# Hybrid decoder step: five early block results held in DRAM, sums of x built sooner, sixteen two-block groups where there were fifteen

## The chip, the cores and the metric

One core of a Trainium2 chip runs one launch of the kernel. The metric is device time in microseconds (us), the median of the runs; less is better. The engines are called as in the profile: PE does matmuls, DVE, ACT and POOL do elementwise work, SP issues most DMAs. Each engine takes its own instructions strictly in the order written in the program.

## The reference, cut to what matters

A prompt of 16 meta tokens and 512 new tokens and a group of 8 single-token samples pass through one layer with shared weights: 536 token columns, 2048 features.

```python
xn = rmsnorm(x, norm_gain)
h = jnp.einsum('btd,de->bte', xn, w_in)
q, k, v, z_a, u, z_s, g_a, g_s = jnp.split(h, IN_SPLITS, axis=-1)
# q, k, v -> sliding-window attention with sinks -> o_attn;  u -> S5 state space scan, gelu, GLU -> y_ssm
br_a = (o_attn * jax.nn.silu(z_a)) @ w_attn_out
br_s = (y_ssm * jax.nn.silu(z_s)) @ w_ssm_out
return x + (jax.nn.sigmoid(g_a) * br_a + jax.nn.sigmoid(g_s) * br_s) @ w_out
```

All is float32. The change touches how the 48 blocks of 128 features of g_s (numbers 0 to 15), z_s (16 to 23), z_a (24 to 31) and g_a (32 to 47) are computed, and in which order.

## The kernel before, in words

**Split matmuls.** Each float32 operand is split in a high and a low part (`whi`, `wlo`, `xh`, `xl`), and a product is three matmuls: high by high, high by low, low by high. A weight *unit* is 1024 input features by 128 output features, 512 KB: SP loads `raw`, ACT casts `whi`, DVE subtracts `wlo`. The token columns come as two halves of 260 (268 with the meta columns), so each matmul streams 260 columns.

**Plain blocks and groups.** A plain block (`xblock`, `mm`) is two units: 2 units, 8 slices, 3 products, 2 halves, 96 matmuls of 260 columns. A group (`Quads`, `quad`) computes two blocks by a Strassen-like scheme: 7 products of 8 slices by 3, 168 matmuls of 260 columns, where two plain blocks take 192. It needs sums of the weights (made on DVE, line 1073) and sums of the halves of x (`tau`, made by `taus`: x is loaded again as `xg`, scaled on ACT, added up in `T` on DVE, then cast on ACT and subtracted on DVE, eight times).

**Stages.** (1) While x and the first weights arrive, PE computes the first three blocks together (line 1255); ACT squares x for the norm. (2) A chain of small steps makes the row scale `R`: PE sums the squares (`wg<-ones,acc`), DVE takes an inverse square root (lines 559 to 564), writes five small diagonal matrices `dg`, PE spreads each with a matmul against ones, DVE copies `R`. Meanwhile PE goes on with two more blocks. The results of these five early blocks stay in SBUF (`keep`, the tiles `xr` of the pool `xld`) until `R` is there; then `evac` multiplies them by `R`, applies the gate function (for 16 to 31: a tanh on ACT and one more DVE step) and writes them to `gD` in DRAM. (3) Four plain blocks (`NA`). `taus` runs beside them. (4) Fifteen groups (`NQ`). (5) `ORDER1`: one plain block, then eight blocks of u and twelve of q, k and v in turn, with the state space scan beside them on DVE, ACT and PE. (6) Seven plain blocks, then a last one that is written out apart, with attention beside them; (7) the GLU, the two branch products, the output product in eight groups.

**What sets the order.** `XORDER` says which block is computed when. Side work is a set of generators (`bg.add`), of which a few steps are written after every few matmuls. A scheduler then fixes the order on each engine at build time; `high_priority` pulls steps forward. The tiles `z` and `t` of the pool `ev` are rings of two buffers each: a third `z` waits until the DMA that reads the first has ended. The weights run through rings of three `raw`, three `whi` and three `wlo`.

Of the kernel before, what the change touches and what calls it, by code (L numbers as in the profile page):

```python
# [8 lines left out]
F32 = mybir.dt.float32  # L9
# [544 lines left out]
def rsqrt_dve(nc, pool, out, v_, shape, tag, end="t", iters=3):  # L554

    v = nc.vector
    t = pool.tile(shape, F32, name=tag + end)
    oi, vi = out.bitcast(I32), v_.bitcast(I32)
    v.tensor_scalar(out=oi, in0=vi, scalar1=1, scalar2=None, op0=ALU.arith_shift_right)
    v.tensor_scalar(out=oi, in0=oi, scalar1=-1.0, scalar2=1597463007.0, op0=ALU.mult, op1=ALU.add)  # L560
    for _ in range(iters):
        v.tensor_tensor(out=t, in0=v_, in1=out, op=ALU.mult)
        v.scalar_tensor_tensor(out=t, in0=t, scalar=-0.5, in1=out, op0=ALU.mult, op1=ALU.mult)  # L563
        v.scalar_tensor_tensor(out=out, in0=t, scalar=1.5, in1=out, op0=ALU.add, op1=ALU.mult)
# [111 lines left out]
class Attn:  # L676
# [228 lines left out]
    def sample(self, oD):  # L905
# [14 lines left out]
        for e in range(2):  # L920
# [168 lines left out]
def trunk(tc, A, O):  # L1089
# [89 lines left out]
    def mm_x(w0, **kw):  # L1179
        return mm(2, lambda k, c: xk(xh, k, c, w0), lambda k, c: xk(xl, k, c, w0), w0, **kw)  # L1180
# [26 lines left out]
        nc.sync.dma_start(out=gD[i], in_=flat(z))  # L1207


    with tc.tile_pool(name="xld", bufs=2, side="right") as xld:  # L1210
        ones = xld.tile([P, P], F32, name="ones", bufs=1)
        v.memset(ones, 1.0)

        wt = aux.tile([P, 512], F32, name="tr")
        for _ in range(NWARM):
            nc.tensor.matmul(wt[:, 0:P], lhsT=ones, rhs=ones, start=True, stop=True)
        acc = xld.tile([P, 2, CH], F32, name="acc", bufs=1)
        def square(kt):
            sq = acc if kt == 0 else xld.tile([P, 2, CH], F32, name="xsq")
            nc.scalar.activation(out=sq, in_=xrs[kt], func=AF.Square)  # L1220
            if kt:
                v.tensor_tensor(out=acc, in0=acc, in1=sq, op=ALU.add)

        def keep(i, ps):

            t = xld.tile([P, 2, CH], F32, name="xr", bufs=NXR)
            with tc.high_priority(offset=HIGH):
                nc.scalar.copy(out=t[:, :, 0:260], in_=ps)
            early.append((i, t[:, :, 0:260]))

        xrs, early = [], []
        NB0 = 3
        ps3 = [aux.tile([P, 2, 512], F32, name="aux")] + [mmp.tile([P, 2, 512], F32, name="mm") for _ in range(2)]
        gain = cst.tile([P, 16], F32, name="gain")
        pieces = {0: 1, 1: 1, 2: 2, 4: 4, 8: 4, 12: 4}
        for kt in range(16):
            xr = xld.tile([P, 2, CH], F32, name="xr", bufs=NXR)
            xrs.append(xr)
            nc.sync.dma_start(out=xr, in_=A["x"][:, kt])
            if kt == 0:  # L1240
                nc.sync.dma_start(out=gain, in_=A["gain"])
            if kt % 8 == 0:
                first = ws.made
                w3 = [ws.tiles(first + j) if kt == 0 else ws.tiles(first + j, xld) for j in range(NB0)]
                ws.made = ws.i = first + NB0
            kp = xkeep(kt, xr, None)
            next(kp)
            for j in range(NB0):
                if kt in pieces:
                    ws.piece(first + j, w3[j], slice(kt % 8, kt % 8 + pieces[kt]))  # L1250
            next(kp)
            for (_, wh, wl), ps in zip(w3, ps3):
                for (wt, xo, f, l) in ((wh, xh, kt == 0, False), (wh, xl, False, False), (wl, xh, False, kt == 15)):
                    for c in range(2):
                        nc.tensor.matmul(ps[:, c, 0:260], lhsT=wt[:, kt % 8], rhs=xk(xo, kt, c, 8), start=f, stop=l)  # L1255
# [4 lines left out]
        early.sort(key=lambda e: e[0])  # L1260
        square(14)
        square(15)
        idn = const("idn")

        af = acc.rearrange("p c w -> p (c w)")
        rp = [aux.tile([P, 512], F32, name=n) for n in ("tr", "wg")]
        toks = [(i, 128 * i, min(128, 2 * CH - 128 * i)) for i in range(5)]
        var = xld.tile([P, 5], F32, name="var", bufs=1)
        rt = xld.tile([P, 5], F32, name="rt", bufs=1)
        v.memset(var, 1.0)  # L1270
        for i, t0, n in toks:
            nc.tensor.matmul(rp[1][0:n, 32 + i:33 + i], lhsT=af[:, t0:t0 + n], rhs=ones[:, 0:1], start=True, stop=True)
        for sl, n in ((slice(0, 4), P), (slice(4, 5), 24)):
            v.tensor_scalar(out=var[0:n, sl], in0=rp[1][0:n, 32 + sl.start:32 + sl.stop], scalar1=1.0 / 2048, scalar2=1e-6,
                            op0=ALU.mult, op1=ALU.add)
        rsqrt_dve(nc, xld, rt, var, [P, 5], "rx")
        Rf = R_.rearrange("p c w -> p (c w)")
        for i, t0, n in toks:
            dg = xld.tile([P, P], F32, name="dg")
            v.tensor_scalar(out=dg[0:n, 0:n], in0=idn[0:n, 0:n], scalar1=rt[0:n, i:i + 1], scalar2=None, op0=ALU.mult)  # L1280
            nc.tensor.matmul(rp[i // 4][:, t0 % 512:t0 % 512 + n], lhsT=ones[0:n], rhs=dg[0:n, 0:n], start=True, stop=True)
        v.tensor_copy(out=Rf[:, 0:512], in_=rp[0])
        v.tensor_copy(out=Rf[:, 512:536], in_=rp[1][:, 0:24])
        for i in range(NB0, NB0 + 2):
            keep(i, mm_x(8))
        for i, t in early:
            evac(XORDER[i], t)
        nx = NB0 + 2
    C = {"idn": idn}
    e32, dsk, bglu, smc = const("e32"), const("dsk"), const("bglu"), const("smc")  # L1290

# [142 lines left out]
        step()  # L1434


    tauc = tc.tile_pool(name="tau", bufs=1, side="right")
    tau = tauc.__enter__()
    tbc = tc.tile_pool(name="tb", bufs=1, side="right")
    tb = tbc.__enter__()  # L1440
    tt = [tau.tile([P, 2, 4, 260], F32R, name=f"tau{p}") for p in range(8)]

    def taus():
        xgs = []

        def load(p):
            if p < 8:
                xgs.append(tb.tile([P, 2, 2, CH], F32, name="xg", bufs=4))
                with tc.issue_after(bg.last):
                    nc.sync.dma_start(out=xgs[p], in_=A["x"][:, 2 * p:2 * p + 2])  # L1450

        for p in range(3):
            load(p)
        yield 0.0
        for p in range(8):
            load(p + 3)
            xg = xgs[p]
            for k in range(2):
                nc.scalar.activation(out=xg[:, k], in_=xg[:, k], func=AF.Copy, scale=gain[:, 2 * p + k:2 * p + k + 1])
            T = tb.tile([P, 4, 260], F32, name="T", bufs=2)  # L1460
            b = xg.rearrange("p k c w -> p (k c) w")[:, :, 8:CH]
            v.tensor_tensor(out=T[:, 0:3:2], in0=b[:, 0:4:3], in1=bc(b[:, 1], 1, 2), op=ALU.subtract)
            v.scalar_tensor_tensor(out=T[:, 1], in0=T[:, 0], scalar=-1.0, in1=b[:, 3], op0=ALU.mult, op1=ALU.subtract)
            v.tensor_tensor(out=T[:, 3], in0=T[:, 1], in1=b[:, 2], op=ALU.add)
            nc.scalar.copy(out=tt[p][:, 0], in_=T)
            yield 1.6
            v.tensor_tensor(out=tt[p][:, 1], in0=T, in1=tt[p][:, 0].bitcast(F32), op=ALU.subtract)
            yield 1.2
    bg.add(taus())
    qs = Quads(tc, nc, A["w"], ws.i + 2 * NA, NQ, wp, 3, 2)  # L1470
    ws.limit = qs.first
    for i in range(NA):
# [357 lines left out]
def _layout(i):  # L1830
# [28 lines left out]
    n0 = 5 + NA  # L1859
# [90 lines left out]
```

## Time and profile before

| what | before |
|---|---|
| median of 3 runs | 1264.08 us (1263.49 to 1266.17) |
| span of the profiled execution | 1262.3 us |
| PE busy | 1250.9 us, 99% |
| DVE busy | 980.6 us, 78% |
| ACT busy | 628.7 us, 50% |
| HBM traffic over the span | 173 GB/s |

For the profiled execution the page gives the span, first to last instruction; a run's time holds in addition what lies around the span. Matmuls are pipelined: the duration of one (283 ns in mean in the groups) is its way through the array, and the next starts long before it ends. What a matmul costs is the distance from start to start, which a row of the chain of waits gives as its length over its count.

### The profile page before, as it was taken

The page shows a single profiled execution, that of the slowest core. Times are in us where ns is not written, and L with a number is a line of the kernel's source. Part 1 is how long each engine was busy: PE and PEld are TensorE (multiplying, and loading weights), DVE is VectorE, ACT ScalarE, POOL GpSimd, SP SyncE. Part 2 cuts the span into 40 slices and gives each one's busy share as a digit, 9 for nine tenths or more (in the row PEclk, how much of TensorE's full clock was granted, in tenths as well). Part 3 has the DMA queues.
Part 4 walks back from the last instruction along what each step waited for, and adds up shares of the span by engine and source line. Part 5 has one row for each costly group of instructions (what it writes and reads, how often), then busy time and mean ns, then how long its engine had stood idle before and what let it go on. Part 6 is the DMA issues. An engine that isn't in the chain of part 4 may idle for free.

```text
span 1262.3 us, 26537 instructions
## 1 busy us (share of the span) xinstructions
PE 1250.9 (99%) x10357; PEld 1227.7 (97%) x10357; DVE 980.6 (78%) x1554; ACT 628.7 (50%) x1344; POOL 266.1 (21%) x437
## 2 busy tenths in 40 slices
PE   9999999999999999999999999999999999999998
PEld 9999999999999999999999999999999999999998
DVE  8687878887778668888897377899887577887875
ACT  8554445444545586556432235567555333344342
POOL 0003999940000033122220123211011000000000
PEclk9999999999999999999999989999999999999999
DMA  8544343443434656555554775777666756555441
GB/s 294 199 160 153 134 143 110 143 150 134 151 126 146 214 172 182 159 165 167 156 159 121 246 211 182 224 240 225 189 214 203 258 174 189 165 192 163 145 139 51
DMA packets 108001, 219.22 MB, mean 174 GB/s; under 512 B 21932, under 2 KB 47492, under 8 KB 107844
## 3 DMA queue, kind: packets, MB, share of 16 engines
q1 hardware_dynamic: 99172, 198.53, 48.5%
q0 software_dynamic: 8704, 19.00, 5.6%
q8 instruction: 81, 1.33, 0.4%
q14 instruction: 44, 0.36, 0.1%
HBM read 181.57 MB, written 36.82 MB: 173 GB/s over the span
## 4 chain that ended last, share of the span: by engine, by line
PE 92%; DVE 3%; DMA 2%; ACT 1%; SPq 1%; issue 0%; DVEq 0%; ACTq 0%
PE mm L1168 45%; PE pr L1382 35%; PE wg L854 2%; PE mm L1255 2%; PE aux L1382 1%; PE aux L1168 1%; PE aux L1255 1%; DVE wlo L1009 1%; PE aux L806 1%; PE aux L805 1%; ACT ct L346 1%; PE tr L526 1%; PE tr L836 1%; PE wg L526 1%; DMA Y<-yD 0%
## 5 line engine op out<-in xcount | busy, mean ns | idle before, releaser
L1075 DVE TENSOR_TENSOR wlo<-raw,whi 128x1024 fp32r<-128x1024 f32 x161 | 198.5, 1253 | 69.6 <-ACT whi L1074 69.0
L1074 ACT CAST whi<-raw 128x1024 fp32r<-128x1024 f32 x161 | 166.4, 1049 | 167.2 <-DVE raw L1073 80.0
L1168 PE MATMUL mm<-xh,whi 128*128 128x260 f32 (+1 forms) x792 | 185.8, 288 | 3.1 <-DVE t L563 2.9
L1008 ACT CAST whi<-raw 128x1024 fp32r<-128x1024 f32 (+3 forms) x128 | 122.3, 965 | 132.3 <-PE mm L1168 85.6
L1168 PE MATMUL mm<-xh,wlo 128*128 128x260 f32 (+1 forms) x792 | 184.4, 287 | 0.0
L1168 PE MATMUL mm<-xl,whi 128*128 128x260 f32 (+1 forms) x792 | 184.1, 286 | 0.0
L1009 DVE TENSOR_TENSOR wlo<-raw,whi 128x1024 fp32r<-128x1024 f32 (+3 forms) x128 | 142.2, 1119 | 46.5 <-ACT whi L1008 45.7
L1382 PE MATMUL pr<-tau,whi 128*128 128x260 f32 x928 | 168.6, 283 | 0.0
L1382 PE MATMUL pr<-cb,whi 128*128 128x260 f32 x848 | 153.0, 283 | 0.0
L1382 PEld LDWEIGHTS pr<-tau,whi 128*128 128x128 f32 x928 | 143.0, 188 | 0.0
L1168 PEld LDWEIGHTS mm<-xh,whi 128*128 128x128 f32 x792 | 132.5, 189 | 5.8 <-ACT KH L747 3.1
L1168 PEld LDWEIGHTS mm<-xl,whi 128*128 128x128 f32 x792 | 133.1, 190 | 0.4 <-issue 0.4
L1168 PEld LDWEIGHTS mm<-xh,wlo 128*128 128x128 f32 x792 | 132.2, 189 | 0.4 <-issue 0.4
L1382 PEld LDWEIGHTS pr<-cb,whi 128*128 128x128 f32 x848 | 130.8, 188 | 0.2 <-ACT z L1416 0.2
L1382 PE MATMUL pr<-tau,wlo 128*128 128x260 f32 x464 | 130.8, 282 | 0.0
L1382 PE MATMUL pr<-cb,wlo 128*128 128x260 f32 x424 | 119.1, 283 | 0.2 <-DVE wlo L1075 0.2
L1073 DVE TENSOR_TENSOR raw<-raw 128x1024 f32<-128x1024 f32 x91 | 113.9, 1252 | 1.6
L1168 PE MATMUL mm<-Y,whi 128*128 128x260 f32 x576 | 105.1, 287 | 0.0
L1382 PE MATMUL pr<-xl,whi 128*128 128x260 f32 x352 | 98.9, 283 | 0.0
L1382 PE MATMUL pr<-xh,wlo 128*128 128x260 f32 x352 | 98.8, 283 | 0.0
L1382 PE MATMUL pr<-xh,whi 128*128 128x260 f32 x352 | 97.1, 283 | 0.0
L1382 PEld LDWEIGHTS pr<-tau,wlo 128*128 128x128 f32 x464 | 87.2, 188 | 0.0
(421 smaller groups left out, 2974.9 us busy)
## 6 DMA issues: line engine op xcount, KB each, us to landing
raw<-in_w SPq DMA_DIRECT2D x202, 512.0 KB, 4.3
gD<-z SPq DMA_DIRECT2D x34, 260.0 KB, 4.3
t<-gD SPq DMA_DIRECT2D x32, 260.0 KB, 3.1
cache<-in_vc POOLq DMA_DIRECT2D x16, 286.0 KB, 3.5
cache<-in_kc POOLq DMA_DIRECT2D x15, 288.0 KB, 4.0
xr<-in_x SPq DMA_DIRECT2D x16, 268.0 KB, 6.5
xg<-in_x SPq DMA_DIRECT2D x8, 536.0 KB, 4.7
sbw<-rawD SPq DMA_DIRECT2D x16, 260.0 KB, 5.1
```

What stands on the lines that cost most here:

```text
L346: nc.scalar.activation(out=dst, in_=src, func=AF.Copy, scale=x)
L526: nc.tensor.matmul(o[n], lhsT=D["CL"][:, 2 * e + n, i, 1:5], rhs=H[:, 2 * e + n, i, 0:140], start=False, stop=(i == 1))
L805: nc.tensor.matmul(ps[:, e, 0:272], lhsT=q, rhs=KH[:, k0:k0 + 272], start=True, stop=False)
L854: nc.tensor.matmul(pv[64 * e:64 * e + 64, 0:256], lhsT=V, rhs=pr[:, e::2], start=(i == 0), stop=(i == len(parts) - 1))
L1008: nc.scalar.copy(out=hi, in_=raw)
L1009: self.dve = nc.vector.tensor_tensor(out=lo, in0=raw, in1=hi.bitcast(F32), op=ALU.subtract).ins
L1073: nc.vector.tensor_tensor(out=o, in0=o, in1=i, op=ALU.add)
L1074: nc.scalar.copy(out=hi, in_=t)
L1075: nc.vector.tensor_tensor(out=lo, in0=t, in1=hi.bitcast(F32), op=ALU.subtract)
L1168: m = nc.tensor.matmul(ps[:, c, 0:W], lhsT=wt[:, k], rhs=xo(kt, c), start=f, stop=l)
L1255: nc.tensor.matmul(ps[:, c, 0:260], lhsT=wt[:, kt % 8], rhs=xk(xo, kt, c, 8), start=f, stop=l)
L1382: m = nc.tensor.matmul(bank, lhsT=wt[:, p], rhs=x(p, e), start=first and f and p == 0, stop=l and p == 7, skip_group_check=not first and l ...
```

## The change

Three things are changed together.

1. **The five early results go to DRAM.** `keep` copies a result into a `z` or `t` tile of `ev` and writes it to a new DRAM tensor `eD`. They are read back, scaled and gated in stage 5, one before each of the second to the sixth item of `ORDER1`.
2. **`taus` comes sooner.** Its pools open after the first three blocks, so it is written beside the two blocks of stage 2. The pool `xld` closes there; the small tiles of the norm are now in a pool `xsm` with one buffer each, also `dg`, which had two.
3. **The blocks are dealt out anew.** Two plain blocks in stage 3 (`NA` 2 for 4), sixteen groups (`NQ` 16 for 15). Five early blocks and nine late plain blocks stay as many as before; the late ones are now 23 to 31, where they were 25 to 31, 46 and 47.

```diff
-NA, NQ = 4, 15
-XORDER = (list(range(16, 25)) + list(range(16)) + list(range(32, 16 + 2 * NQ)) + list(range(25, 32))
-          + list(range(16 + 2 * NQ, 48)))
+NB0, NB1, NA, NQ = 3, 2, 2, 16
+XORDER = list(range(16, 23)) + list(range(16)) + list(range(32, 48)) + list(range(23, 32))
...
+    early = []
+    eD = dram.tile([NB0 + NB1, P, 520], F32, name="eD")
+    xsc = tc.tile_pool(name="xsm", bufs=1)
...
         def keep(i, ps):
-            t = xld.tile([P, 2, CH], F32, name="xr", bufs=NXR)
+            t = ev.tile([P, 2, 260], F32, name="zt"[i % 2])
             with tc.high_priority(offset=HIGH):
-                nc.scalar.copy(out=t[:, :, 0:260], in_=ps)
-            early.append((i, t[:, :, 0:260]))
+                nc.scalar.copy(out=t, in_=ps)
+                nc.sync.dma_start(out=eD[i], in_=flat(t))
+            early.append(i)
...
+    tauc = tc.tile_pool(name="tau", bufs=1, side="right")
...
+    bg.add(taus())        # moved here, unchanged, from ahead of the NA blocks; the norm's chain now follows it
...
-        for i, t in early:
-            evac(XORDER[i], t)
...
     for n_, (kind, n) in enumerate(ORDER1):
+        if n_ and early:
+            i = early.pop(0)
+            z = ev.tile([P, 2, 260], F32, name="z")
+            nc.sync.dma_start(out=flat(z), in_=eD[i])
+            evac(XORDER[i], z, z)
```

The instructions that the two kernels issue differ by this: PE 10008 to 9984 (192 matmuls fewer in plain blocks, 168 more in groups); DVE 1556 to 1566 (four more sums of weights, three more `wlo`, three more steps on group results); ACT 1281 to 1288; SP 704 to 714 (five writes of `eD`, five reads); POOL the same 442.

Where the order moves, before and now. On DVE, in stage 2 of the kernel before: the last step of the inverse square root, the five `dg`, the copies of `R`, the early results.

```order
L564 SCALAR_TENSOR_TENSOR rt<-rxt,rt 128x5
L1280 TENSOR_SCALAR dg<-k_idn,rt 128x128 x2
L1009 TENSOR_TENSOR wlo<-raw,whi 128x1024
L1280 TENSOR_SCALAR dg<-k_idn,rt 128x128 x2
L1280 TENSOR_SCALAR dg<-k_idn,rt 24x24
L1282 COPY R<-tr 128x512
L1009 TENSOR_TENSOR wlo<-raw,whi 128x1024
L1283 COPY R<-wg 128x24
L1200 TENSOR_TENSOR z<-xr,R 128x520 x2
L1206 SCALAR_TENSOR_TENSOR z<-t,z 128x520 x2
```

The same place of the changed kernel, up to the second `dg` (its lines 1294 to 1299 are `taus`, 1318 is `dg`):

```order
L564 SCALAR_TENSOR_TENSOR rt<-rxt,rt 128x5
L1294 TENSOR_TENSOR T<-xg 128x2x260
L1295 SCALAR_TENSOR_TENSOR T<-T,xg 128x260
L1318 TENSOR_SCALAR dg<-k_idn,rt 128x128
L1295 SCALAR_TENSOR_TENSOR T<-T,xg 128x260
L1296 TENSOR_TENSOR T<-T,xg 128x260
L1008 TENSOR_TENSOR wlo<-raw,whi 128x1024
L1296 TENSOR_TENSOR T<-T,xg 128x260
L1299 TENSOR_TENSOR tau_618<-T,tau_618 128x1040
L1318 TENSOR_SCALAR dg<-k_idn,rt 128x128
```

The chain to `R` is now threaded through the work of `taus`, and the scaling of the early results has left this place.

On PE, the first `dg` matmuls among the matmuls of the fourth block, before:

```order
L1168 MATMUL mm<-xh,whi 128x260 x2
L1168 MATMUL mm<-xl,whi 128x260 x2
L1281 MATMUL tr<-dg,ones 128x128 x2
L1168 MATMUL mm<-xh,wlo 128x260 x2
L1168 MATMUL mm<-xh,whi 128x260
```

And now, in the fifth block:

```order
L1167 MATMUL mm<-xhq,whi 128x260
L1167 MATMUL mm<-xl,whi 128x260
L1319 MATMUL tr<-dg,ones 128x128
L1167 MATMUL mm<-xlq,whi 128x260
L1167 MATMUL mm<-xh,wlo 128x260
```

The five stood at the 374th (two), 397th (two) and 420th place of PE's order; they stand at the 439th, 470th, 505th, 534th and 558th, each apart from the next. The first three blocks end at the 298th place in both.

On SP, at the start of `ORDER1`, the loads for the scan (`f`, `bN`, `c`, `B`), weights and results, before:

```order
L1007 DMA raw<-in_w 128x1024
L333 DMA bN<-in_bN 128x256
L331 DMA f_5587<-FD 32x2x512 x3
L1207 DMA gD<-z 128x520
L331 DMA f_5587<-FD 32x2x512
L1007 DMA raw<-in_w 128x1024
L335 DMA c<-in_cT 128x256
L1007 DMA raw<-in_w 128x1024
```

And now (its line 1558 reads an early result back, 1206 writes a gated one):

```order
L1006 DMA raw<-in_w 128x1024
L1558 DMA z<-eD 128x520
L333 DMA bN<-in_bN 128x256
L331 DMA f_5578<-FD 32x2x512 x3
L1006 DMA raw<-in_w 128x1024
L331 DMA f_5578<-FD 32x2x512
L1206 DMA gD<-z 128x520
L1558 DMA z<-eD 128x520
L1006 DMA raw<-in_w 128x1024
L1206 DMA gD<-z 128x520
```

Reads of `eD`, each of which needs a free `z`, now stand between the weight loads.

More of the change, by code (lines that the diff above doesn't have):

```diff
@@ L1207, in evac @@
         nc.sync.dma_start(out=gD[i], in_=flat(z))
+    early = []
+    eD = dram.tile([NB0 + NB1, P, 520], F32, name="eD")
+    xsc = tc.tile_pool(name="xsm", bufs=1)
+    xsm = xsc.__enter__()
     with tc.tile_pool(name="xld", bufs=2, side="right") as xld:
-        ones = xld.tile([P, P], F32, name="ones", bufs=1)
+        ones = xsm.tile([P, P], F32, name="ones")
         v.memset(ones, 1.0)
@@ L1259, in trunk @@
             keep(j, ps3[j][:, :, 0:260])
-        early.sort(key=lambda e: e[0])
+        early.sort()
         square(14)
         square(15)
[L1263 to L1285, printed above, removed]
-        for i, t in early:
-            evac(XORDER[i], t)
-        nx = NB0 + 2
+    idn = const("idn")
+    tauc = tc.tile_pool(name="tau", bufs=1, side="right")
+    tau = tauc.__enter__()
+    tbc = tc.tile_pool(name="tb", bufs=1, side="right")
+    tb = tbc.__enter__()
+    tt = [tau.tile([P, 2, 4, 260], F32R, name=f"tau{p}") for p in range(8)]
@@ new lines, in taus, with load @@
+    def taus():
+        xgs = []
+        def load(p):
+            if p < 8:
+                xgs.append(tb.tile([P, 2, 2, CH], F32, name="xg", bufs=4))
+                with tc.issue_after(bg.last):
+                    nc.sync.dma_start(out=xgs[p], in_=A["x"][:, 2 * p:2 * p + 2])
+        for p in range(3):
+            load(p)
+        yield 0.0
+        for p in range(8):
+            load(p + 3)
+            xg = xgs[p]
+            for k in range(2):
+                nc.scalar.activation(out=xg[:, k], in_=xg[:, k], func=AF.Copy, scale=gain[:, 2 * p + k:2 * p + k + 1])
+            T = tb.tile([P, 4, 260], F32, name="T", bufs=2)
+            b = xg.rearrange("p k c w -> p (k c) w")[:, :, 8:CH]
+            v.tensor_tensor(out=T[:, 0:3:2], in0=b[:, 0:4:3], in1=bc(b[:, 1], 1, 2), op=ALU.subtract)
+            v.scalar_tensor_tensor(out=T[:, 1], in0=T[:, 0], scalar=-1.0, in1=b[:, 3], op0=ALU.mult, op1=ALU.subtract)
+            v.tensor_tensor(out=T[:, 3], in0=T[:, 1], in1=b[:, 2], op=ALU.add)
+            nc.scalar.copy(out=tt[p][:, 0], in_=T)
+            yield 1.6
+            v.tensor_tensor(out=tt[p][:, 1], in0=T, in1=tt[p][:, 0].bitcast(F32), op=ALU.subtract)
+            yield 1.2
@@ new lines, in trunk @@
+    bg.add(taus())
+    af = acc.rearrange("p c w -> p (c w)")
+    rp = [aux.tile([P, 512], F32, name=n) for n in ("tr", "wg")]
+    toks = [(i, 128 * i, min(128, 2 * CH - 128 * i)) for i in range(5)]
+    var = xsm.tile([P, 5], F32, name="var")
+    rt = xsm.tile([P, 5], F32, name="rt")
+    v.memset(var, 1.0)
+    for i, t0, n in toks:
+        nc.tensor.matmul(rp[1][0:n, 32 + i:33 + i], lhsT=af[:, t0:t0 + n], rhs=ones[:, 0:1], start=True, stop=True)
+    for sl, n in ((slice(0, 4), P), (slice(4, 5), 24)):
+        v.tensor_scalar(out=var[0:n, sl], in0=rp[1][0:n, 32 + sl.start:32 + sl.stop], scalar1=1.0 / 2048, scalar2=1e-6,
+                        op0=ALU.mult, op1=ALU.add)
@@ new lines, in trunk @@
+    rsqrt_dve(nc, xsm, rt, var, [P, 5], "rx")
+    Rf = R_.rearrange("p c w -> p (c w)")
+    for i, t0, n in toks:
+        dg = xsm.tile([P, P], F32, name="dg")
+        v.tensor_scalar(out=dg[0:n, 0:n], in0=idn[0:n, 0:n], scalar1=rt[0:n, i:i + 1], scalar2=None, op0=ALU.mult)
+        nc.tensor.matmul(rp[i // 4][:, t0 % 512:t0 % 512 + n], lhsT=ones[0:n], rhs=dg[0:n, 0:n], start=True, stop=True)
+    v.tensor_copy(out=Rf[:, 0:512], in_=rp[0])
+    v.tensor_copy(out=Rf[:, 512:536], in_=rp[1][:, 0:24])
@@ L1289, in trunk @@
+    for i in range(NB0, NB0 + NB1):
+        keep(i, mm_x(8))
+    xsc.__exit__(None, None, None)
+    nx = NB0 + NB1
     C = {"idn": idn}
@@ L1434, in quad @@
         step()
[L1437 to L1469, printed above, removed]
     qs = Quads(tc, nc, A["w"], ws.i + 2 * NA, NQ, wp, 3, 2)
```

7 lines of the change are left out of this document (3 added, 4 removed).

## Prediction

> **What bounds the kernel now.** I read the page's busy times first, then the list of what PE waited for, then the chain of waits, then the busy times by stretch for the two places that the change touches.
>
> ```profile
> span 1262.3 us, 26537 instructions
> PE 1250.9 (99%) x10357; PEld 1227.7 (97%) x10357; DVE 980.6 (78%) x1554; ACT 628.7 (50%) x1344; POOL 266.1 (21%) x437
> ```
>
> PE has work for all but 11.4 us of the span, so time is won by fewer matmuls or lost by new waits of PE. What PE waited for, in total, times, longest:
>
> ```profile
> PE mm L1168 <- DVE t L563: 2.9, 1, 2.9
> PE tr L1216 <- DVE var L1270: 1.1, 1, 1.1
> PE wg L854 <- ACT pm L842: 0.8, 1, 0.8
> PE aux L1255 <- ACT whi L1008: 0.6, 1, 0.6
> PE tr L526 <- DVE H L512: 0.6, 1, 0.6
> PE aux L1349 <- DVE sst L486: 0.6, 1, 0.6
> PE tr L523 <- DVE sst L486: 0.5, 1, 0.5
> PE pr L1382 <- DVE wlo L1075: 0.2, 1, 0.2
> PE mm L1168 <- ACT xr L1228: 0.2, 1, 0.2
> ```
>
> None of these belongs to the `dg` matmuls (line 1281), and three (lines 526, 1349, 523: 0.6 + 0.6 + 0.5 = 1.7 us) belong to the scan of stage 5. The chain of waits, start and length of a piece, shows the three stretches that matter: the start of the two blocks of stage 2, plain blocks, groups:
>
> ```profile
> 41.84 2.90 PE mm L1168 x22
> 57.85 55.62 PE mm L1168 x464
> 113.47 2.87 PE aux L1382 x24
> 139.10 191.59 PE pr L1382 x1594
> ```
>
> A matmul costs 55.62 / 464 = 0.1199 us in plain blocks and 191.59 / 1594 = 0.1202 us in groups: the same, so a group costs what its matmuls cost, and nothing in it waits.
>
> **The change, part by part.**
>
> *One more group for one more pair.* A plain pair is 192 x 0.1199 = 23.02 us, a group 168 x 0.1202 = 20.19 us: 2.83 us less. This lies on PE, which sets the end, all of it. A record may be missing in a piece, which would make both prices about 1% too high: 0.03 us.
>
> *More work on weights.* A group needs seven more DVE steps than a pair, and three more casts on ACT. The busy times by stretch, for each engine, cover it (after PE and PEld come DVE, ACT and POOL, then the granted clock, the DMA share and GB/s):
>
> ```profile
> 200.00:500.00 300.00, 300.00 (x2500) 298.39 (x2499) 232.42 (x294) 165.93 (x361) 85.30 (x129) 1.00 0.47 155
> ```
>
> Groups and the start of stage 5 run with DVE at 232.42 of 300 and PE without idle time. Cost 0; the cover goes if a group's DVE work passes 20.2 us.
>
> *Sums of x sooner, two plain blocks fewer ahead of the groups.* The work itself, line by line, mean ns of one, in the stretch from 30 us to the groups:
>
> ```profile
> L1009 DVE TENSOR_TENSOR wlo<-raw,whi 128x1024 fp32r<-128x1024 f32 (+1 forms) x13 | 14.1, 1096 | 5.3 <-ACT whi L1008 5.3
> L1467 DVE TENSOR_TENSOR tau<-T,tau 128x1040 fp32r<-128x1040 f32 x8 | 9.8, 1238 | 1.0 <-ACT tau L1465 1.0
> L1465 ACT CAST tau<-T 128x1040 fp32r<-128x1040 f32 x8 | 8.4, 1059 | 7.3 <-DVE T L1464 7.3
> L1462 DVE TENSOR_TENSOR T<-xg 128x520 f32<-128x520 f32 x8 | 5.5, 691 | 0.0
> L1206 DVE SCALAR_TENSOR_TENSOR z<-t,z 128x520 f32<-128x520 f32 x8 | 5.5, 696 | 1.0 <-ACT t L1205 0.9
> L1205 ACT ACTIVATE t<-z 128x520 f32<-128x520 f32 x8 | 5.1, 638 | 8.2 <-DVE z L1200 8.2
> L1200 DVE TENSOR_TENSOR z<-xr,R 128x520 f32<-128x520 f32 x5 | 3.4, 697 | 3.3 <-DMA gD<-z 3.3
> L1464 DVE TENSOR_TENSOR T<-T,xg 128x260 f32<-128x260 f32 x8 | 3.2, 421 | 0.0
> L1463 DVE SCALAR_TENSOR_TENSOR T<-T,xg 128x260 f32<-128x260 f32 x8 | 3.2, 420 | 0.0
> ```
>
> On DVE `taus` is 9.8 + 5.5 + 3.2 + 3.2 = 21.7 us, and it must be done when the groups begin. They begin two blocks, 23.0 us, sooner: at 113.5 - 23.0 = 90.5 us. What DVE has there before:
>
> ```profile
> 40.00:64.00 24.00, 23.79 (x198) 23.38 (x197) 11.40 (x32) 10.32 (x15) 0.00 (x0) 1.00 0.42 141
> 64.00:88.00 24.00, 24.00 (x204) 24.00 (x203) 19.27 (x27) 12.83 (x17) 0.00 (x0) 1.00 0.53 179
> 88.00:112.00 24.00, 24.00 (x204) 24.00 (x203) 18.18 (x22) 9.87 (x11) 0.00 (x0) 1.00 0.47 155
> ```
>
> 48.9 us from 40 to 112. It loses five results scaled (5 x 1.39 = 7.0 us), two blocks of weights (four `wlo` at 1.22, of which the line above has 13 with one shorter form: 4.9 us) and two results (2.8 us at most). Some 34 us remain for the 50 us from 40 to 90.5. ACT has 33.0 us there before, and no less room. Cost 0: the sums are ready ahead of the groups. If that cover were gone, the groups' first weights would be late next.
>
> *The chain to `R`, one `dg` at a time.* With one buffer the second `dg` waits on DVE until PE has used the first, and PE's order holds each `dg` matmul at a fixed place. The matmuls stand 141, 172, 207, 236 and 260 places behind the end of the first three blocks; from 41.84 us on, at 0.12 us and with a microsecond for the ten sums of squares, PE comes to the first at about 59.6 us. Adding the rows above in DVE's new order (two `tau`, two `T`, the small steps, one `wlo`, two `tau`, one and a half `T`) brings DVE to the first `dg` at about 57.5 us, and to the later ones some 1.5 us ahead of PE: an estimate from these rows. Bounds: 0 (none of the five waits before), or, if DVE is late by one `wlo` at each of the four that wait for a buffer, 4 x 1.22 = 4.9 us. A gain is excluded, since there is no wait to take away. I take 0, as the estimate has slack at each. `R` is then ready at about 75 us; the first block that needs it ends at 76 us, and a second PSUM buffer gives 11 us more.
>
> *Five results scaled in stage 5.* 7.0 us of DVE, 5 x 0.64 = 3.2 us of ACT, and ten DMAs of 260 KB, five of them new reads. What these engines do there:
>
> ```profile
> 430.00:450.00 20.00, 20.00 (x170) 19.32 (x169) 12.77 (x22) 19.30 (x75) 4.77 (x9) 1.00 0.69 238
> 450.00:470.00 20.00, 20.00 (x165) 20.00 (x164) 12.62 (x31) 19.35 (x69) 2.87 (x6) 1.00 0.57 177
> 470.00:490.00 20.00, 20.00 (x174) 19.65 (x174) 18.71 (x35) 9.52 (x26) 6.51 (x12) 1.00 0.61 176
> ```
>
> DVE has 14.6 us free from 430 to 470, enough. ACT has 1.3 us: here 3.2 us of tanh push back the casts and the scan's constants by about 2 us, until ACT is half idle from 470 on. Who waits is the scan, whose matmuls are placed a few microseconds later too (the first that needs the scan's result by 16 of 0.12 us, later ones by up to 52, 6 us). Bounds: the three waits of 1.7 us vanish (-1.7), or ACT's 3.2 us reach PE in full (+3.2). I take 0, nearest to the row of 430 to 450, where ACT is full already and PE waits for nothing.
>
> *SP's queue.* A read of `eD` needs a free `z`, and in the order it stands right behind the write that empties another. Issue to landing, the last number:
>
> ```profile
> raw<-in_w SPq DMA_DIRECT2D x202, 512.0 KB, 4.3
> gD<-z SPq DMA_DIRECT2D x34, 260.0 KB, 4.3
> ```
>
> So the read may hold SP 4.3 us, with a weight load behind it. A unit lasts PE 48 x 0.12 = 5.8 us and the ring holds three: 17.3 us from one use of a buffer to the next, less 4.3 for the load and 2.3 for cast and subtraction leaves 10.7 us. One hold is covered, two are; three in a row are not. Cost 0, upper end 3 x 4.3 - 10.7 = 2.2 us. The first gate read of attention now needs the late blocks 24 and 25; it is one more such hold, much later, with the same cover.
>
> **What a wait would cost.** The stretch that holds two of the scan's waits of 0.6 us, the one long wait of PE, and the chain behind it:
>
> ```profile
> 600.00:650.00 50.00, 48.79 (x412) 47.62 (x411) 43.93 (x100) 20.09 (x57) 7.62 (x14) 1.00 0.54 160
> 738.00:742.00 4.00, 1.06 (x7) 0.89 (x7) 2.84 (x9) 3.57 (x13) 1.77 (x4) 0.82 0.92 323
> 742.00:746.00 4.00, 4.00 (x20) 4.00 (x20) 3.90 (x12) 1.22 (x2) 2.40 (x5) 0.50 0.96 235
> 746.00:750.00 4.00, 4.00 (x30) 4.00 (x29) 3.46 (x10) 0.10 (x1) 0.34 (x1) 0.83 1.22 292
> 734.96 4.08 DMA rb<-rkD
> 741.40 22.15 PE mm L1168 x161
> ```
>
> DVE stood in line for a read from DRAM (`rb`), a result of PE was not taken away, PE idled 2.9 us; the granted clock then fell to 0.50, and 161 matmuls took 22.15 us for 161 x 0.12 = 19.3. The wait cost 2.9 + 2.8 = 5.7 us. The waits of 0.6 us between 600 and 650 us cost no clock (1.00). DVE's and SP's rows at this place are in the same order in both kernels, so I let this wait stand.
>
> [...]
>
> **Sum.** -2.83 on PE, 0 elsewhere. The profiled execution would have a span of 1259.5 us. The median of the runs, 1264.08, stands 1.8 us above the span, which I carry over: 1261.3 us, 0.22% less. About 0.2%, 2.5 us, can be told from no change: below 1261.55 is faster, above 1266.6 slower. The forecast lies just past that bound.
>
> **The rivals.**
>
> *Small new waits.* The scan of stage 5 or the `dg` matmuls make PE wait 1 to 3 us in pieces under a microsecond or so, each too short for the clock. For it: ACT at 19.3 of 20, one `dg` buffer. Against: stage 5 absorbs DVE and ACT queues now with 1.7 us of waits. 1262.3 to 1264.3 us, say 1263.2: the same.
>
> *A long wait with the clock behind it.* In the first items of `ORDER1` DVE or SP stands in line for a read of `eD` as it does now for `rb`, and a result or a weight is late by more than the cover of 10.7 us. Price 5.7 us: 1261.3 + 5.7 = 1267.0 us, slower. It decides once PE waits so long that wait and clock pass 5.3 us together. For it: the rows at 738 show the mechanism. Against: there the chain is two DRAM trips one after the other, here one.
>
> *The group gains nothing.* `taus` ends late and the first group starts late by what it saves: 1264.1 us. For it: the time ahead shrinks by 23 us. Against: 34 us of work for 50.
>
> *Old waits go.* The new order drops the scan's waits, or the one at 741: 1261.3 - 1.7 = 1259.6, or 1255.6 us. For it: that order is made anew in stage 5. Against: the rows around 741 stay.
>
> **How the numbers follow.** The forecast 0.50, the small waits 0.27, the long wait 0.10, no gain 0.06, old waits gone 0.07. Faster: the last and nine tenths of the forecast (its own range, 1260.3 to 1262.0, reaches over the bound): 0.07 + 0.45 = 0.52. Slower 0.10. The same: 0.38. The range 1258.6 to 1265.0 holds the forecast, the small waits, no gain and the lesser half of the old waits, and leaves out the long wait and 1255.6.
>
> **What would show it.** After: 2688 matmuls in groups at 0.12 us; the groups begin at about 90.5 us; no wait at the `dg` line (1319); the scan's waits near 1.7 us; the wait at the key rows again near 738 us, 2.8 us sooner; one dip of the clock. Wrong if PE waits at line 1319 or in stage 5 for over 1 us in all, or if there is a second dip or none.

## The result, and the profile after

The changed kernel takes 1280.05 us (median of 4 runs, 1274.66 to 1281.99), beside 1265.08 us for the kernel before on the same chip: ratio 1.0114, 95% interval 1.009 to 1.0138. It is slower by 1.1%, some 14 to 15 us, where the forecast was 0.2% faster. The profiled execution took 1279.43 us, with a span of 1277.7 us. One of the four runs of e8 below took 5921.47 us where the other three took 1270.94 to 1273.45, and its ratio is without that run (its median of 1272.67 us is with it).

Where the time went is read best from matmuls that both kernels issue once, in the same place of the program. The rows give first and last start. Four of them, before: the groups of stage 4, the first step of attention (line 771, after stage 5), the last plain block (`mm<-xh,whi`), the output product.

```profile
L1382 PE MATMUL pr<-tau,whi x928: 277/282/293, 116.2 to 419.9; 128*128 128x260 f32 x186
L771 PE MATMUL tr<-k_idn,vb x8: 272/273/273, 724.5 to 728.4; 128*128 128x128 f32 x8
L1693 PE MATMUL mm<-xh,whi x24: 277/282/384, 817.2 to 827.6; 128*128 128x260 f32 x24
L1382 PE MATMUL pr<-cb,whi x848: 277/282/387, 1098.7 to 1258.1; 128*128 128x260 f32 x170
```

After:

```profile
L1419 PE MATMUL pr<-tau,whi x992: 277/283/293, 93.0 to 414.6; 128*128 128x260 f32 x199
L771 PE MATMUL tr<-k_idn,vb x8: 270/272/274, 736.7 to 740.6; 128*128 128x128 f32 x8
L1702 PE MATMUL mm<-xh,whi x24: 278/283/367, 829.3 to 839.5; 128*128 128x260 f32 x24
L1419 PE MATMUL pr<-cb,whi x848: 277/283/388, 1114.2 to 1273.6; 128*128 128x260 f32 x170
```

The groups end sooner (part of the 5.3 us between their last rows is that less of the next block is mixed into the last group; without that part it is 3.0 us). Attention starts 12.2 us later although the groups are done 3.0 us sooner, so stage 5 lost about 15 us. The last block ends 11.9 us later, and the output product starts 15.5 us later: another 3.6 us went in the stage between. Two places, then.

What PE waited for, after:

```profile
PE aux L391 <- ACT s L346: 3.7, 1, 3.7
PE mm L1167 <- DVE t L563: 3.3, 1, 3.3
PE tr L469 <- DVE g L540: 3.0, 3, 1.6
PE wg L854 <- ACT pp L846: 1.2, 1, 1.2
PE aux L805 <- DVE S L811: 1.1, 1, 1.1
PE tr L1219 <- DVE var L1308: 1.1, 1, 1.1
PE wg L523 <- DVE sst L486: 1.0, 1, 1.0
```

The second row is the old wait. Lines 391, 469 and 523 are the scan of stage 5: 3.7 + 3.0 + 1.0 = 7.7 us where it was 1.7. The stretches shown of before, after (PE, PEld, DVE, ACT, POOL, granted clock, DMA share, GB/s):

```profile
430.00:450.00 20.00, 16.28 (x126) 15.07 (x125) 15.09 (x25) 16.88 (x60) 5.03 (x10) 0.89 0.68 203
450.00:470.00 20.00, 20.00 (x155) 20.00 (x155) 8.23 (x16) 17.17 (x63) 2.04 (x4) 0.94 0.72 215
470.00:490.00 20.00, 20.00 (x165) 18.98 (x165) 19.07 (x40) 13.43 (x45) 7.06 (x13) 1.00 0.58 160
```

126 and 155 matmuls where there were 170 and 165, with a dip of the clock that before did not have (0.11 and 0.06 of 20 us, together 3.4 us of clock). The chain of waits leads back from line 391:

```profile
434.69 0.60 DVE B L375
435.30 0.61 DVE z L1199
435.91 0.62 DVE z L1205
436.53 0.02 issue
436.55 4.13 DMA gD<-z
440.67 0.02 issue
440.69 3.22 DMA z<-eD
443.91 0.03 issue
443.93 0.02 DVEq L1199
443.95 0.04 issue
444.00 0.26 DVE z L1199
444.26 0.90 ACT s L346 x4
445.17 0.53 ACT t L1204
445.69 0.43 ACT s L346 x2
446.13 0.60 PE aux L391 x2
```

The second read of `eD` needs a free `z`. It waits until the write that empties that `z` has landed (4.13 us), then takes 3.22 us itself. DVE's own rows there, with idle time and its releaser in brackets:

```profile
439.88 0.71 DVE L1590 TENSOR_TENSOR uf<-mm,R 128x536 f32<-128x536 f32 x1
444.00 0.70 DVE L1199 TENSOR_TENSOR z<-z,R 128x520 f32<-128x520 f32 x1 [3.41 <-DMA z<-eD]
444.62 0.69 DVE L1205 SCALAR_TENSOR_TENSOR z<-t,z 128x520 f32<-128x520 f32 x1
445.23 0.68 DVE L381 TENSOR_TENSOR CL<-ct,ct 128x512 f32<-128x512 f32 x1
```

DVE stands still for 3.41 us in front of a scaling that nobody needs soon, and behind it stands `CL`, which line 391 on PE does need. Before, DVE made `CL` 2.6 us sooner:

```profile
442.63 0.69 DVE L381 TENSOR_TENSOR CL<-ct,ct 128x512 f32<-128x512 f32 x1 [1.09 <-ACT ct L346]
```

PE itself comes to line 391 at 442.4 us, where before it came at 445.1, so the lateness of `CL` meets an earlier PE. The chain and the list name `s` of ACT as what released line 391, but line 391 multiplies `bb` by `CL`: the first half of `CL` ends at 445.91 us, 0.21 us before PE starts, and in e10 below it is 0.21 us again (444.13 and 444.34). Over stage 5 the list of DVE's waits has this row:

```profile
DVE z L1199 <- DMA z<-eD: 10.8, 4, 4.7
```

A third part of the loss is in no list of waits. The 128 matmuls of line 391 stood in 9 pieces between the matmuls of the blocks; now they stand in 18. PE's busy time on them from 400 to 740 us (PE, PEld), before and after:

```profile
400.00:740.00 340.00, 5.71 (x128) 3.30 (x128) 1.00 0.57 173
```

```profile
400.00:740.00 340.00, 11.41 (x128) 6.21 (x128) 0.99 0.61 174
```

That is 5.7 us more, a little of it from the dip (the two pieces there took 1.56 us up to the next other matmul, 0.92 before). So stage 5's 15 us are about 6.0 us of new waits (7.7 less 1.7), 3.4 us of clock and up to 5.7 us for line 391; the parts overlap a little.

### The profile page after: what moved, and what is told of

Its sections match the earlier page's. It is cut to its first block, busy times and chain, and to the rows that moved or that the text cites. A ratio compares the mean times of both kernels' runs of the same rounds, so it can differ in the third digit from the quotient of the medians.

```text
span 1277.7 us, 26525 instructions
## 1 busy us (share of the span) xinstructions
PE 1258.5 (99%) x10333; PEld 1232.0 (96%) x10333; DVE 989.0 (77%) x1564; ACT 633.4 (50%) x1351; POOL 265.4 (21%) x437
## 4 chain that ended last, share of the span: by engine, by line
PE 83%; DMA 6%; DVE 5%; ACT 4%; SPq 1%; issue 1%; DVEq 0%; ACTq 0%
PE mm L1167 38%; PE pr L1419 37%; PE wg L854 1%; PE aux L1419 1%; DVE wlo L1008 1%; DMA c<-in_cT 1%; ACT whi L1007 1%; DMA kD<-k 1%; ACT ct L346 1%; DMA f<-FD 1%; DMA z<-gD 1%; PE mm L1702 1%; PE aux L805 1%; PE aux L806 1%; PE tr L469 1%
## 5 line engine op out<-in xcount | busy, mean ns | idle before, releaser
L1074 DVE TENSOR_TENSOR wlo<-raw,whi 128x1024 fp32r<-128x1024 f32 x168 | 207.1, 1252 | 70.9 <-ACT whi L1073 68.7
L1073 ACT CAST whi<-raw 128x1024 fp32r<-128x1024 f32 x168 | 173.9, 1050 | 177.0 <-DVE raw L1072 78.1
L1419 PE MATMUL pr<-tau,whi 128*128 128x260 f32 x992 | 180.1, 283 | 0.0
L1167 PE MATMUL mm<-xh,whi 128*128 128x260 f32 (+1 forms) x744 | 174.2, 288 | 3.5 <-DVE t L563 3.3
L1167 PE MATMUL mm<-xh,wlo 128*128 128x260 f32 (+1 forms) x744 | 175.3, 288 | 0.0
L1167 PE MATMUL mm<-xl,whi 128*128 128x260 f32 (+1 forms) x744 | 174.8, 289 | 0.0
L1419 PEld LDWEIGHTS pr<-tau,whi 128*128 128x128 f32 x992 | 152.9, 188 | 0.0
L1419 PE MATMUL pr<-tau,wlo 128*128 128x260 f32 x496 | 139.9, 283 | 0.0
L1167 PEld LDWEIGHTS mm<-xh,whi 128*128 128x128 f32 x744 | 125.1, 190 | 5.1 <-ACT KH L747 3.5
L1167 PEld LDWEIGHTS mm<-xl,whi 128*128 128x128 f32 x744 | 125.7, 191 | 0.8 <-issue 0.8
```

Of the source, the lines that this page charges most:

```text
L1073: nc.scalar.copy(out=hi, in_=t)
L1074: nc.vector.tensor_tensor(out=lo, in0=t, in1=hi.bitcast(F32), op=ALU.subtract)
L1167: m = nc.tensor.matmul(ps[:, c, 0:W], lhsT=wt[:, k], rhs=xo(kt, c), start=f, stop=l)
L1419: m = nc.tensor.matmul(bank, lhsT=wt[:, p], rhs=x(p, e), start=first and f and p == 0, stop=l and p == 7, skip_group_check=not first and l ...
```

## The experiments

The theory after this reading: DVE and SP stand in line for the reads of `eD`, and the scan behind them is late. Rivals: the plain amount of added work (7.0 us of DVE, 3.2 us of ACT, ten transfers); the new order of groups and blocks. "+x us" below is the ratio less one, times the kernel before's 1264 us.

**Which part of stage 5.** Scaling left out, reads left out, all left out, reads on another queue.

```diff
 e1_no_scale:    -            evac(XORDER[i], z, z)
                 +            nc.sync.dma_start(out=gD[XORDER[i]], in_=flat(z))
 e2_no_read:     -            nc.sync.dma_start(out=flat(z), in_=eD[i])
                 -            evac(XORDER[i], z, z)
                 +            evac(XORDER[i], R_[:, :, 8:CH])
 e3_nothing:     keep() writes to gD[XORDER[i]]; nothing in ORDER1
 e4_pool_queue:  -            nc.sync.dma_start(out=flat(z), in_=eD[i])
                 +            nc.gpsimd.dma_start(out=flat(z), in_=eD[i])
```

> The changed kernel with the five early results read from eD and written to gD in stage 5 as before, but not scaled on the way (it leaves out their multiplication by R, tanh and gating; the ten DMAs stay). If SP's queue is the cause (a read waits for a free z and holds the scan's loads behind it), nothing changes: 1277 to 1281 us, and PE again waits 3 to 4 us at line 391 with the clock's dip behind it. If DVE's 7.0 and ACT's 3.2 us of scaling are the cause, the time falls to 1262 to 1266 us. If it is the new order of groups and blocks, it stays near 1280 here and in the two runs that follow.

> The changed kernel with the five scalings and their writes to gD at the same places of stage 5, but with R as what they scale instead of a result read back from eD (it leaves out the right values of five blocks; DVE and ACT do the same work, five reads are gone). SP's queue as the cause: 1262 to 1266 us, no wait at line 391. DVE's and ACT's work as the cause: 1277 to 1281 us. Both about equally: near 1271 here and in the run before.

> The changed kernel with the five early results written to gD at once, unscaled, and nothing of them in stage 5 (it leaves out their scaling). Both theories of stage 5: 1260 to 1263 us, the time that the group gain of 2.9 us gives, and PE's waits in stage 5 near the 1.7 us of before. If the new order of groups, sums of x and blocks is the cause: over 1270 us.

> The changed kernel complete, with the five reads of eD issued on the POOL queue instead of SP's. SP's queue as the cause: 1262 to 1268 us, if POOL's own few transfers in stage 5 (the results u on their way to the scan) do not suffer in turn. DVE's and ACT's work as the cause: 1277 to 1281 us.

| run | median us | ratio (95%) | against before |
|---|---|---|---|
| e1, transfers alone | 1269.82 | 1.0047 (1.0031 to 1.0063) | +5.9 us |
| e2, scaling alone | 1269.34 | 1.0039 (1.0024 to 1.0054) | +4.9 us |
| e3, neither | 1264.35 | 1.0008 (0.9991 to 1.0024) | +1.0 us |
| e4, reads on POOL's queue | 1277.13 | 1.0104 (1.0082 to 1.0126) | +13.1 us |

None of the three theories came out alone: e1 and e2 each lie near the 1271 us of "both about equally". Without the five results (e3) some 13 of the 14 us are gone: the loss of stage 5 is theirs, not that of the groups. But transfers alone cost 4.9 us over e3, scaling alone 3.9, and both together 13.4: more than the sum. SP's queue as such is not the main cause, since the reads cost nearly as much from another queue (the intervals of e4 and the changed kernel overlap, and line 391 waits 4.5 us in e4). And the median of e3 is 3 us above the 1261 that the groups' gain should give, though its ten runs spread from 1259.45 to 1270.84.

What e2 lost is not a wait. PE waits 1.5 us for the scan in it, no more than before, the clock of stage 5 is 1.00, and yet attention starts at 727.5 us, where it starts at 722.3 in e3. Line 391 stands in 19 pieces in e2 and takes 11.35 us of PE; in e3 it stands in 12 and takes 6.91. In e2 a piece of 4 to 8 of these matmuls took 0.34 to 0.57 us up to the next other matmul, a piece of 16 took 0.59 (in the changed kernel 0.55 to 0.57 for pieces of 4 and 6, 0.59 for 16), so it is the number of pieces that costs. The order was fixed at build time: work added to DVE and ACT moved the scan's matmuls on PE. Why the scheduler splits them was not tried. In e1 it is the other way round: line 391 keeps its 9 pieces, and PE waits 5.4 us for the scan, with one dip of the clock.

**Is the excess the coupling?** Four runs: the same work with nobody waiting for a read; a wait with hardly any work; each scaling one item behind its read; the start moved past the scan's first constants.

```diff
 e9_uncoupled:    z<-eD, gD<-z as they are; DVE and ACT scale R_ into a t tile
 e10_touch:       e1 and   +  v.tensor_tensor(out=z[:, :, 0:8], in0=z[:, :, 0:8], in1=R_[:, :, 8:16], op=ALU.mult)
 e7_lag:          the evac of an item's read is written after that item
 e12_late_start:  -        if n_ and early:
                  +        if n_ > 5 and early:
```

> The changed kernel with the same ten transfers, and with the same 7.0 us of DVE and 3.2 us of ACT, but uncoupled: the five results go from eD to gD as they are, and DVE and ACT scale R into a buffer that nothing reads (it leaves out the right values of five blocks). DVE waits for no read. If the excess of the two alone (5.5 us of transfers, 5.0 us of work, 15.7 together) is DVE standing in line for the reads: 1273 to 1276 us. If it is two loads that pile up on the same stretch: 1278 to 1281 us.

> The run with ten transfers and no scaling, plus one DVE instruction on 2 x 8 columns of each result between its read and its write (the scaling is left out). It adds under 0.5 us of DVE work in all, but DVE's line now waits for the reads as in the changed kernel. If standing in line is a cost of its own: 1273 to 1276 us, with DVE waiting about 10 us for z from eD. If only the amount of work counts: 1269 to 1271 us, as without the touch.

> The changed kernel complete, with each scaling one item of ORDER1 behind its read: the read is issued before the item, DVE's multiplication stands behind the item's own work, some 11 us later. The same ten transfers, the same 7.0 us of DVE and 3.2 us of ACT. If the loss is DVE standing in line for the reads (it waited 10.8 us in all for z from eD): no such wait, and 1268 to 1273 us. If it is the amount of work and traffic alone: 1277 to 1281 us.

> The changed kernel complete, with the five reads and scalings begun at the seventh item of ORDER1 instead of the second, past the scan's first constants. If the wait of 3.7 us at line 391 and the clock's dip (some 6 us) come from the second read standing ahead of the scan's first constants on DVE: 1272 to 1275 us, no wait at 442 us and no dip there. If the load only moves to a stretch as full (DVE has 1 us free in 20 after 500 us): 1278 to 1282 us.

| run | median us | ratio (95%) | against before |
|---|---|---|---|
| e9, uncoupled | 1272.23 | 1.0057 (1.004 to 1.0074) | +7.2 us |
| e10, touch | 1273.25 | 1.0068 (1.0049 to 1.0087) | +8.6 us |
| e7, lag | 1276.55 | 1.0097 (1.0083 to 1.0111) | +12.3 us |
| e12, late start | 1269.92 | 1.0053 (1.0034 to 1.0072) | +6.7 us |

With the same transfers and the same work but no instruction of DVE behind a read (e9), 7 us of the 14 are gone, a little more than was forecast for standing in line, and with them PE's wait at 442 us and the dip there. This is no clean price of standing in line: line 391 is down to 11 pieces (6.70 us), and PE waits elsewhere instead, 5.2 us at line 526 and 2.4 at line 391 later on. The stretch from 430 to 450 us in e9:

```profile
430.00:450.00 20.00, 19.70 (x166) 18.98 (x166) 14.26 (x24) 17.64 (x64) 5.89 (x11) 1.00 0.77 231
```

The touch (e10) brings the wait back with under half a microsecond of work: line 391 is in 9 pieces as before, DVE waits 12.5 us in front of the touches, PE waits 2.7 us at line 391 (the list names no releaser, only issue) and does 136 matmuls from 430 to 450 us at a granted clock of 0.91, and the time is inside the range forecast for standing in line; its interval overlaps that of e1, so the price of the touch alone, 2.7 us, is not settled. The lag (e7) was to take DVE's waits away and did not; the scheduler fixes DVE's order anew, and its list of DVE's waits reads nearly as that of the changed kernel:

```profile
DVE z L1199 <- DMA z<-eD: 10.6, 2, 7.7
```

So e7 tells nothing against the theory and little for it. In e12 the work is all there and so are some waits (5.7 us of DVE for `z<-eD`), but past the scan's first constants; PE does 161 matmuls from 430 to 450 us at full clock, and 7.7 us come back, more than forecast (line 391 is in 14 pieces, 8.48 us):

```profile
430.00:450.00 20.00, 19.10 (x161) 18.36 (x161) 13.15 (x22) 20.00 (x74) 5.61 (x11) 1.00 0.63 194
```

About 6 us over e3 are left in e9 and in e12, in new waits of PE in the scan and, in e12, in the pieces of line 391: stage 5 has no slack for the work and the traffic even where no read holds up the scan's first constants.

**The first part alone.** The kernel before, with only the five results changed (`eD`, scaled in `ORDER1`).

> The kernel before with the five results alone changed: they go to eD unscaled and are read, scaled and written in the items of ORDER1; four plain blocks, fifteen groups, sums of x and order of blocks as before. If the whole loss of 14 to 15 us in stage 5 is made there: 1277 to 1282 us. If it takes the new groups' end (an odd number of groups, which leaves the other buffers busy) as well: 1268 to 1274 us.

1272.67 us, ratio 1.006 (1.0041 to 1.0078), +7.6 us: the early results alone make it slower, about half of the whole loss. The expectation's second case holds in its number. There DVE waits for the second read only 0.48 us, and line 391 starts at 445.6 us without a wait, half a microsecond later than before. Its loss is elsewhere: line 391 is in 18 pieces (10.77 us), and PE waits 3.2 us at line 523. In the changed kernel PE comes to line 391 3.2 us sooner than in e8, but DVE begins on the scan's load `B` (line 372) only 1.9 us sooner (430.2 and 432.1 us), so the slack ahead of line 391 is 1.3 us less. Why the load lags there was not tried.

**The other 3 us: the late blocks.** e3 lost its 3 us in one place. From 850 to 870 us, before and in e3:

```profile
850.00:870.00 20.00, 20.00 (x167) 19.19 (x167) 19.75 (x37) 14.83 (x36) 6.02 (x8) 1.00 0.77 246
```

```profile
850.00:870.00 20.00, 17.58 (x130) 16.21 (x129) 18.73 (x38) 13.78 (x36) 1.76 (x5) 0.91 0.81 245
```

37 matmuls fewer, and a dip of the clock. Two runs put the old order of blocks back, one in e3, one in the complete kernel:

```diff
-XORDER = list(range(16, 23)) + list(range(16)) + list(range(32, 48)) + list(range(23, 32))
+XORDER = list(range(16, 25)) + list(range(16)) + list(range(32, 46)) + list(range(25, 32)) + [46, 47]
```

> The run with nothing of the five results in stage 5 (they go to gD unscaled, so their scaling is left out), with the order of blocks of before: 16 to 24, 0 to 15, 32 to 45, 25 to 31, 46, 47, so that 23 and 24 are in a group and 46 and 47 come late again. That run ended 3 us later than the group gain explains, and lost it from 858 to 872 us, in the gating after the last block. If the new late blocks cause this, the time is 1260 to 1262 us here, 3 us less, with no wait of PE at 861 us. If something else does (a group more, the sums of x sooner), it stays at 1263 to 1265.

> The changed kernel complete, with the order of blocks of before (23 and 24 in a group, 46 and 47 late). If the late blocks cost 3 us apart from stage 5: 1276 to 1278 us, and the gating after the last block takes as long as before. If the two losses share a cause: 1279 to 1281 us.

e5: 1261.19 us, ratio 0.9986 (0.9974 to 0.9997), which is 2.8 us better than e3 (the intervals overlap a little). e11: 1273.02 us, ratio 1.0066 (1.0043 to 1.0089), 6 us better than the changed kernel and better than both forecasts. In the profile of e11, its slowest run, stage 5 is as bad as ever, and from the last block to the output product nothing is lost (830.1 to 1110.4 us is 280.3, before 281.5, changed kernel 284.9), which explains some 4.6 of the 6 us:

```profile
L1702 PE MATMUL mm<-xh,whi x24: 277/282/384, 830.1 to 839.7; 128*128 128x260 f32 x24
L1419 PE MATMUL pr<-cb,whi x848: 277/283/389, 1110.4 to 1269.8; 128*128 128x260 f32 x170
```

**A version that beats both.** The reads and scalings go into groups, where DVE is busy 15.6 of 20 us and ACT half; the old order of blocks stays. A group with `y` in `z` leaves the ring of `t` free:

```diff
+            if nst == 1 and q >= 4 and q % 2 == 0 and early:
+                i = early.pop(0)
+                z = ev.tile([P, 2, 260], F32, name="t")
+                nc.sync.dma_start(out=flat(z), in_=eD[i])
+                evac(XORDER[i], z, z)
```

> The changed kernel complete, but the five results are read back, scaled and written in the groups 4, 6, 8, 10 and 12 (in the ring of t, which such a group does not use), and the blocks are in the order of before. DVE has 2 to 4 us free in each 20 us there. If stage 5's engines and queues are the cause and the late blocks the rest: 1260 to 1263 us, faster than both kernels. If stage 5 suffers from something else in this change: over 1270.

1260.2 us, ratio 0.9975 (0.9965 to 0.9985): faster than both kernels, the output product 4.3 us sooner than before. It is also no slower than e5, which leaves the scaling out (the intervals overlap), so in the groups the five results cost nothing that shows. In its profile stage 5 keeps two small waits of the scan:

```profile
PE mm L1167 <- DVE t L563: 3.3, 1, 3.3
PE tr L1219 <- DVE var L1308: 1.1, 1, 1.1
PE aux L391 <- ACT z L1389: 0.9, 1, 0.9
PE tr L526 <- DVE H L512: 0.6, 1, 0.6
```

With stage 5 quiet, the late blocks can be looked at by themselves: the same kernel in the change's order, and in a mixed order (24 in the first group, 25 as the plain block of `ORDER1`, then 23, 26 to 31, and 47 last).

> The run with the five results scaled in the groups, but in the order of blocks of the change (23 to 31 late). Stage 5 is as in that run, so only the late blocks differ. If they cost 3 us after the last plain block whatever happens in stage 5: 1263 to 1264 us, lost between 830 and 905 us. If they cost nothing once stage 5 is undisturbed: 1260 to 1261 us.

> The same with 24 moved into the first group, 25 the first late block, and 47 the last (23 and 26 to 31 between). The gate read of attention's first heads then waits for no late block, but seven gated blocks (one DVE operation of 0.7 us more each) still follow stage 5. If the 3 us come from that gate read being 55 to 70 us later: 1260 to 1261 us, the read issued near 700 us again. If they come from the gated blocks' extra work on DVE: 1263 to 1264 us.

e13: 1263.86 us, ratio 1.0005 (0.9994 to 1.0017). The new order costs 3.8 us there, more than the gain of the group, again from 850 to 870 us, where the chain of waits runs through DVE's steps of attention and of the gating (857 to 862 us):

```profile
850.00:870.00 20.00, 17.62 (x131) 16.27 (x131) 18.32 (x37) 14.30 (x39) 1.46 (x4) 0.91 0.78 245
```

e14: 1263.68 us, ratio 0.9996 (0.9986 to 1.0006), no better by an amount that counts, although attention's first gate read is at 703.8 us again (759.8 in e13, 702.7 before). So that gate read is not the cause by itself. A gated block more among the late ones fits, but PE's waits lie elsewhere in e14 (830 to 870 us, without a dip), so how the order makes DVE late there stays open.

## Why the prediction was wrong, point by point

- **The group, -2.83 us: right.** The groups begin at 90.3 us (forecast 90.5), a piece of 1594 matmuls again takes 191.59 us, and PE is through with them 3.0 us sooner. e5 and e6 show it as time, -1.8 and -3.2 us, with 2.8 inside both intervals.

```profile
90.31 2.87 PE aux L1419 x24
115.94 191.59 PE pr L1419 x1594
```

- **Sums of x sooner, one `dg` buffer, weight work: right.** No row of PE's waits has line 1319, and no group waits. In this kernel these parts cost nothing.
- **Five results scaled in stage 5, cost 0 with an upper end of 3.2 us: the step that failed.** It took DVE's free time from 430 to 470 us, 14.6 us, as room for 7.0 us of work. But part of DVE's free time is waiting for the scan's own inputs (before, 1.09 us for `ct` right ahead of `CL`), and a scaling put in front of `CL` brought its wait (3.41 us) there as well as its work (1.2 us): `CL` began at 445.23 us, before at 442.63. The runs give 3.9 us for the scaling alone (e2 less e3), already over the upper end, and 6 to 13 with the reads. The bounds counted waits and ACT's work alone; that the order on PE is made anew, and line 391 with it (18 pieces for 9, up to 5.7 us), was no term of the sum, although the rival of old waits going says that the order is made anew in stage 5. Taking "nearest to the row of 430 to 450, where ACT is full already and PE waits for nothing" was the choice that made it 0: a row without waits shows that the slack was enough for the old work, not how much is left.
- **SP's queue, cost 0, upper end 2.2 us: mis-sized, and counted for the wrong victim.** The cover of 10.7 us was that of the weights, and PE waited for no weight over 0.2 us in stage 5. Late were the scan's steps behind the scaling on DVE. Transfers alone cost 4.9 us (e1 less e3).
- **The rival that came true: "DVE or SP stands in line for a read of `eD`", with 0.10.** Its place (the first items of `ORDER1`), its order of events and its price are in the trace: 3.7 us of wait and up to 3.4 us of clock, where it gave 5.7. It is about half of stage 5's loss. The argument against it, "there the chain is two DRAM trips one after the other, here one", failed: there are two here as well, the write that frees `z` (4.13 us) and the read (3.22 us). The prediction had the order (a read right behind the write that empties another `z`) and 4.3 us for such a transfer in its part on SP's queue, and did not add them up on DVE. It also priced one such wait, where five results come one per item and DVE waited four times, 10.8 us.
- **Late blocks, "one more such hold, much later, with the same cover", cost 0: failed.** The order of blocks costs 3 to 4 us by itself (e13 against e6, e3 against e5). The gate read, which the prediction named, is not what costs it (e14).
- **Old waits unchanged: right.** The wait at the key rows is there (3.3 us), later by what stage 5 lost. The one dip of the clock that the prediction named became three, at 446, 753 and 879 us.

## What to carry to other kernels

Free time of an engine in a stage full of dependent steps is not room: ask what stands behind the new instruction in that engine's order, and how long the instruction's own input takes from the moment its buffer comes free, the write that frees it included. Optional work with a DRAM round trip belongs where engines have slack against a long, independent stream, here the groups, and not ahead of a chain that feeds PE. Where a stage loses more than its new waits and its dip add up to, compare the busy time of the same instructions in both kernels: line 391 took twice as long (11.41 us for 5.71) without any wait. A gain of 3 us must also be checked against every reordering that comes with it: here the order of nine blocks ate it whole.

## What the runs showed of the hardware that was not expected

The same wait of PE at the key rows, 2.2 to 3.6 us long, cost the clock by steps. In the profiled runs of before (wait 2.9 us) and of the changed kernel (3.3 us) the granted clock fell to 0.50 long enough to lose 3.4 us of clock each; in twelve of the experiments, with waits of 2.9 to 3.6 us, it lost 1.7 us; in e7 and e13, with waits of 2.2 and 2.8 us, nothing. Twice 1 - 0.84, 1 - 0.50 and 1 - 0.81 is 1.7 us, in e6:

```profile
738.00:740.00 2.00, 0.49 (x2) 0.52 (x3) 1.97 (x7) 1.93 (x8) 1.14 (x4) 0.84 0.84 215
740.00:742.00 2.00, 2.00 (x11) 2.00 (x10) 1.94 (x9) 1.44 (x2) 1.56 (x4) 0.50 0.94 269
742.00:744.00 2.00, 2.00 (x16) 2.00 (x15) 1.97 (x6) 0.00 (x0) 0.95 (x2) 0.81 1.10 249
```

What makes steps of it is not shown: the twelve short dips come to 1.70 to 1.72 us of clock each, the two long ones to 3.42, twice that. The wait's length alone does not decide between them: 2.9 us went with 3.4 us of clock in the kernel before and with 1.7 in e1 and e12, and the longest waits, 3.6 us in e3 and e5, went with 1.7. The dip can begin before the wait ends, as in the first row above, where PE is busy 0.49 of 2 us and the granted clock is already 0.84 in mean, and that part costs nothing. So by an estimate from the wait and the part of the dip behind it, one such wait cost 2.2 to 2.8 us where no dip followed, 4 to 5.5 us with the short dip and some 6 us with the long one; the forecast's price of 5.7 us came from one execution, at the dear end. What decides between no dip, the short one and the long one is not shown.
